# A ninth pair with seven products in the last output projection of a two-layer encoder, its seventh operand block in the distance table's room

## The chip, the cores and the metric

The kernel runs on one core of a Trainium2 chip. The metric is the device time of one execution in microseconds (us). The kernel before ran three times: 2584.67, 2586.02 and 2587.11 us, the median is 2586.02. One further execution was profiled; it took 2583.95 us, of which the profile's span covers 2581.8.

## What is computed

Two layers (DEPTH = 2) work on 256 tokens with 4096 features. A layer normalises x, projects it with w_in (4096 x 11264), runs attention and retention heads on the result and projects their 4096 outputs with w_out (4096 x 4096) onto x:

```python
for l in range(DEPTH):
    h = rmsnorm(x, norm_w[l])
    proj = h @ w_in[l]
    ...
    x = x + jnp.concatenate([a_out, r_out], axis=-1) @ w_out[l]
return rmsnorm(x, final_norm)
```

The four projections are called phases 0 to 3 here. Phase 3, the last w_out, is the one that the change touches. It is followed only by the residual, the final norm and the store.

## The kernel before, in words

**Pairs and products.** The 4096 rows of a weight are 32 tiles of 128, taken as 16 pairs (0 to 15). A pair times a block of 2 x 512 columns is a 2 x 2 product of blocks (two weight tiles, two halves of the tokens, two column blocks of 512). It is done either with eight block products or, by Strassen's scheme in Winograd's form, with seven. Each block product is three matmuls of 128 x 128 by 512 columns, since every operand is split into a high and a low part: high by high, high weight by low operand, low weight by high operand. The banks M1 to M7 in PSUM collect the products over all pairs of a block; at its end a few VectorE additions (`combining`, tiles `ca` and `cb`) turn them into the output. Phase 3 has four blocks of 1024 columns, called blocks 0 to 3 here. `SEVEN_OUT` (L157) lists the pairs that take seven products in w_out: the even ones, eight of 16.

**What a pair needs.** Its weights come from HBM by SyncE as two transfers of 512 KB into `wraw` (6 buffers). A pair with eight products makes two pages, A and B, of 1024 columns each: ScalarE casts the high part (`whi<-wraw`), VectorE subtracts for the low part (`wlo<-wraw,whi`). Page B of most of them is "far": ScalarE makes `fhi` and the negated `flo`, and a GpSimd transfer adds the weight to `flo`, so that VectorE does nothing for it. A pair with seven products makes four pages, A, T, B, U. T and U are sums of weights that VectorE builds first (`wsum`, one instruction of 1024 columns, then two of 512), and VectorE makes the low parts of all four (`wlo` of 1024 columns for A, T, U, and `wlb` of 512 for B). There are 3 buffers for `wlo`, 4 for `whi`, 2 for `wsum`, one for `whb`/`wlb`.

**The order within a block** (`groups_of`, `pages_of`). A group is a pair with seven products and the pairs with eight that follow it; the pages of both alternate. With the even pairs on seven, each group is one seven and one eight.

**Operands.** The activations of a pair are split once per phase (`split_pair`) into tiles `x7h`/`x7l` (7 blocks of 128 columns), `x8h`/`x8l` (6 blocks, 8 buffers, given out in turn) or `xmh`/`xml` for pair 14. In phase 3 the splits of the later pairs run during block 0, together with the rest of the retention work of layer 1.

**The late pairs and the tail.** `LATE` (L195) is the last four pairs below 15 with eight products: 7, 9, 11 and 13. In block 3 their M4 products are put off to the very end (`rest_units`), 24 matmuls, so that the other banks can be combined meanwhile. The half page that is kept for this lies in the `x8` or `x7` buffer of an earlier pair that is through. When pair `LATE_PAIR` = 5 (L61) and all before it are through in block 3, `after` starts the loads that only the tail needs: two rows of `final_norm` into `x8h` and `x8l`, the buffers after the two that pair 7's half pages took (pair 5's own), and then, in `residuals`, two residual blocks of 512 KB into `wsum`. `last_combining` waits for both residuals before it adds anything but M1, M6 and M7.

**Order of the work.** A recording layer runs through the whole program when it is built, with a clock of its own, and writes down each engine's instruction order. On the chip each engine runs its list strictly in that order and waits on semaphores. `dist` (L431) is a table of token distances that the retention weights read (L1404, L1406), for the last time in phase 2.

Of the kernel before, what the change touches and what calls it, by code (L numbers as in the profile page):

```python
# [12 lines left out]
F32R = mybir.dt.float32r  # L13
# [5 lines left out]
P = 128  # L19
D_MODEL = 4096  # L20
SEQ = 256
DEPTH = 2
# [13 lines left out]
ALL = slice(None)  # L36
# [27 lines left out]
PE_PASS = 0.2  # L64
# [91 lines left out]
SEVEN_IN = (0,2,4,6,8,10,12)  # L156
SEVEN_OUT = (0, 2, 4, 6, 8, 10, 12, 14)  # L157
FAR_IN=(1,3,5,7,9,11,13)
FAR_OUT = (1, 3, 5, 7, 9, 11, 13)
SEVENS = (SEVEN_IN, SEVEN_OUT) * DEPTH  # L160
BORDER_FAR = 10


def fars(phase, b):

    few = (FAR_IN, FAR_OUT)[phase % 2]
    if (b == 0 and phase) or (phase % 2 == 0 and b == N_IN - 1):
        eights = [_p for _p in range(NP) if _p not in SEVENS[phase]]
        return few + tuple(_p for _p in eights if _p not in few)[: BORDER_FAR - len(few)]
    return few  # L170


SEVEN_ALWAYS = sum(_p in SEVEN_IN and _p in SEVEN_OUT for _p in range(NP))
EIGHT_ALWAYS = sum(_p not in SEVEN_IN and _p not in SEVEN_OUT for _p in range(NP))
MIXED = tuple(_p for _p in range(NP) if (_p in SEVEN_IN) != (_p in SEVEN_OUT))
# [47 lines left out]
class Now:  # L223

    t = 0.0
# [121 lines left out]
def hybrid_encoder(  # L347
# [17 lines left out]
    ve = Clock(nc.vector, vector_cost, 0.083, now)  # L365
    ac = Clock(nc.scalar, scalar_cost, 0.098, now)
    pe = Clock(None, None, PE_PASS - PASS, now)
# [8 lines left out]
    cp = ctx.enter_context(tc.tile_pool(name="cp", bufs=1))  # L376
# [14 lines left out]
    def t(pool, shape, tag, bufs=None, dt=F32):  # L391
        kw = {} if bufs is None else {"bufs": bufs}
        return pool.tile(shape, dt, tag=tag, name=tag, **kw)

    def f32(v):
        return v.bitcast(F32)
# [9 lines left out]
    def drop(n=1):  # L406

        held[0] -= n
        own(-n)
# [8 lines left out]
    def page(shape, name, dt=F32):  # L418

        held[0] += 1  # L420
        own(1)
        assert held[0] <= PAGES, (name, now.t, [(v.steps.__name__, v.need, v.own, v.begun) for v in tasks], pledged(), wanted, sums_of)
        return sp.tile(shape, dt, tag="pg", name=name, bufs=PAGES)
# [7 lines left out]
    dist = t(cp, [P, 2 * SEQ], "dist", dt=mybir.dt.bfloat16)  # L431
# [334 lines left out]
    weights = Weights()  # L766
# [157 lines left out]
    operand = [None] * NP  # L924
# [5 lines left out]
            need_at.setdefault((g.phase, g.pair), g.at)  # L930
    plain, plain_left = {}, list(DIRECT)
    late, stored, sums_of, split_of = [], {}, [], {}

    def split_pair(p, v, phase, gains):

        def tokens(v):

            return v.rearrange("p k (a t) -> p k a t", t=BLK)

        x0, x1 = v[:, 0], v[:, 1]  # L940
        if gains is not None:
            yield "A"
            for i in range(2):
                u = v[:, :, i].rearrange("p m a t -> p (a m) t" if phase else "p m a t -> p m (a t)")
                ac.activation(u, u, AF.Copy, scale=gains[i])
        seven = p in SEVENS[phase]
        tag, n = ("xm", len(MIXED)) if p in MIXED else ("x7", SEVEN_ALWAYS) if seven else ("x8", EIGHT_ALWAYS)
        blocks = 6 if tag == "x8" else 7
        if seven:
            yield lambda: not sums_of and held[0] + sum(max(0, v.need - v.own) for v in tasks if v.begun) < PAGES  # L950
            sums_of.append(p)
            hi, lo = (t(ap, [P, blocks, P], tag + s, n, F32R) for s in "hl")
            f = page([P, 5, P], "xf")
            yield "A"
            s1, s2, s3, s4, a22n = (tokens(f)[:, i - S4] for i in (S1, S2, S3, S4, A22N))
            ac.activation(a22n, x1[:, 1], AF.Copy, scale=-1.0)
            ac.copy(tokens(hi[:, 0:2, :]), x0)
            yield "V"
            ve.tensor_sub(s1, a22n, x1[:, 0])
            ve.scalar_tensor_tensor(s2, s1, -1.0, x0[:, 0], op0=ALU.mult, op1=ALU.subtract)  # L960
            ve.tensor_sub(s3, x0[:, 0], x1[:, 0])
            ve.tensor_sub(s4, x0[:, 1], s2)
            yield "A"
            ac.copy(hi[:, 2:7, :], f)
            yield "V"
            ve.tensor_sub(tokens(lo[:, 0:2, :]), x0, tokens(f32(hi)[:, 0:2, :]))
            ve.tensor_sub(lo[:, 2:7, :], f, f32(hi)[:, 2:7, :])
            sums_of.pop()
            drop()
        else:  # L970
            hi, lo = (t(ap, [P, blocks, P], tag + s, n, F32R) for s in "hl")
            u = [w[:, :4].rearrange("p (i m) (a t) -> p i m a t", i=2, t=BLK) for w in (hi, lo)]
            g = [tokens(w[:, 4:6]) for w in (hi, lo)]
            yield "A"
            for i in range(2):
                ac.copy(u[0][:, i], v[:, :, i])
            yield "V"
            for i in range(2):
                ve.tensor_sub(u[1][:, i], v[:, :, i], f32(u[0])[:, i])
            ve.tensor_sub(x0, x0, x1)  # L980
            yield "A"
            ac.copy(g[0], x0)
            yield "V"
            ve.tensor_sub(g[1], x0, f32(g[0]))
        split_of[p // 2] -= 1
        if not split_of[p // 2]:
            drop()
        version[p] = phase
        operand[p] = (hi, lo)
        operand_at[p] = max(ve.done, ac.done)  # L990
# [188 lines left out]
    def at(parts, *index):  # L1179
        return [v[index] for v in parts]  # L1180
# [394 lines left out]
    def block(after_pair, phase, first_order=False, order=LAST_ORDER, last=None):  # L1575
# [37 lines left out]
        for n, (p, k, (bank, index, h), part) in enumerate(units):  # L1613
            if n == len(units) - COMBINE_LEAD:
                wanted[0] = 2
            while (p, k) not in pages:
                g = weights.pages[weights.at]
                weights.at += 1
                assert g.phase == phase
                pages[g.pair, g.kind] = g  # L1620
            g = pages[p, k]

            def ready():
                if part == "D":
                    return (
                        weights.has(g, "raw")
                        and p in plain
                        and plain[p][2 if index[1] == 2 else 1] <= now.t
                        and (n != first[bank] or bank_at[bank] is not None and bank_at[bank] <= now.t)
                    )  # L1630
                when = g.high_at if part == "H" else g.low_at
                if when is None or not (when() if callable(when) else when <= now.t) or version[p] != phase or operand_at[p] > now.t:
                    return False
                return n != first[bank] or (bank_at[bank] is not None and bank_at[bank] <= now.t)

            yield ready
            if n == first[bank]:
                acc[bank] = t(pm, [P, NB], bank)
                bank_at[bank] = None
            if part == "D":  # L1640
                a = None
            elif g.seven:
                a = at(operand[p], *index, ALL)
            else:
                a = at(operand[p], ALL, 4 + index[0] if index[1] == 2 else 2 * index[0] + index[1], ALL)
            if part == "D":
                matmul(acc[bank], plain[p][0][index], f32(g.raw[0])[:, h], n == first[bank], n == final[bank], 4)
            elif part == "H":
                b = g.hi if k == PAGE_B and g.seven else g.hi[h] if last and p in LATE else g.hi[:, h]
                matmul(acc[bank], a[0], b, n == first[bank], False)  # L1650
                matmul(acc[bank], a[1], b, False, False)
            else:
                b = g.lo if k == PAGE_B and g.seven else g.lo[h] if last and p in LATE else g.lo[:, h]
                matmul(acc[bank], a[0], b, False, n == final[bank])
            if n == final[bank]:
                fin[bank] = pe.done
            if n < len(units) - len(rest_units):
                uses[p, k] -= 1
                if not uses[p, k]:
                    weights.release(g)  # L1660
            left[p] -= 1
            if not left[p]:
                done.append(p)
                if last and p not in MIXED and p < NP - 1:
                    weights.holds["x7" if g.seven else "x8"].give(pe.until + PE_PASS)
                if part == "D":
                    plain_left.remove(p)
            while done and all(not left[q] for q in range(min(done))):
                q = min(done)
                done.remove(q)  # L1670
                after_pair(q)
# [378 lines left out]
```

## Time and profile before

| | us |
|---|---|
| median of 3 runs | 2586.02 |
| profiled execution | 2583.95 |
| its span | 2581.8 |
| TensorE busy | 2564.9 |
| VectorE busy | 2317.7 |
| ScalarE busy | 1911.4 |
| GpSimd busy | 443.8 |

"Busy" sums the times in which an engine has an instruction in flight; instructions of one engine overlap a little, so a busy share near 100% can also mean that the next one always starts at once. In a timeline a row is start, duration, engine, source line, instruction, and in brackets the idle time before it and what ended it. L1170 is the line of every matmul and L248 that of every recorded VectorE and ScalarE instruction, so the tiles tell them apart.

### The profile page before, as it was taken

To read this page: it belongs to the slowest core of one execution; us is meant where nothing else is said; L and a number is where in the kernel's file an instruction comes from. 1 tells how busy PE (TensorE), PEld (TensorE's weight loads), DVE (VectorE), ACT (ScalarE), POOL (GpSimd) and SP (SyncE) were. 2 spreads that over 40 slices of the span, in tenths; PEclk is the share of its full clock that TensorE was granted. 3 is DMA by queue.
4 is the path that set the end of the run, shared out by engine and by line. 5 is a ranking of instruction groups with operands and counts; after the bars stand their busy time and mean duration, and the time that the engine had idled before them with its cause. 6 is when DMAs were issued, how large, how long until landed. Compare 5 with 4: busy or idle time off the path is not lost.

```text
span 2581.8 us, 34363 instructions
## 1 busy us (share of the span) xinstructions
PE 2564.9 (99%) x11474; PEld 2115.2 (82%) x11474; DVE 2317.7 (90%) x2911; ACT 1911.4 (74%) x2680; POOL 443.8 (17%) x604
## 2 busy tenths in 40 slices
PE   9999999999999999999999999999999999999998
PEld 5888888888888888888888888888888888888886
DVE  7999988999889899888998989989989888998887
ACT  8877776777777688766887776767778777876665
POOL 0022211221222110111112121212212111101111
PEclk9999999999999999999999999999999999999999
DMA  9999989998998898999999998989998998989987
GB/s 322 306 281 300 287 274 284 282 303 261 287 289 267 278 287 246 291 289 288 305 304 284 291 283 272 276 284 291 293 272 283 283 281 258 291 247 289 268 264 231
DMA packets 212739, 727.53 MB, mean 282 GB/s; under 512 B 25536, under 2 KB 32320, under 8 KB 212560
## 3 DMA queue, kind: packets, MB, share of 16 engines
q1 hardware_dynamic: 146464, 519.21, 56.8%
q0 software_dynamic: 66096, 206.11, 34.7%
q8 instruction: 90, 1.47, 0.2%
q14 instruction: 89, 0.73, 0.1%
HBM read 676.99 MB, written 48.23 MB: 281 GB/s over the span
## 4 chain that ended last, share of the span: by engine, by line
PE 95%; issue 1%; DVE 1%; DMA 1%; ACT 1%; POOL 0%; SPq 0%; POOLq 0%; DVEq 0%; ACTq 0%
PE M L1170 92%; PE ps L1170 3%; DMA full<-in_xT 0%; DVE wlo L248 0%; DMA flo<-in_w_in 0%; DVE wsum L248 0%; ACT whi L248 0%; DVE cb L248 0%; PE ps L1009 0%; DMA wraw<-in_w_in 0%; DVE ca L248 0%; POOL out L1862 0%; ACT full L248 0%; ACT fhi L248 0%; SPq L372 0%
## 5 line engine op out<-in xcount | busy, mean ns | idle before, releaser
L248 ACT CAST whi<-wraw 128x1024 fp32r<-128x1024 f32 (+1 forms) x521 | 540.2, 1045 | 200.5 <-PE M L1170 128.6
L248 DVE TENSOR_TENSOR wlo<-wraw,whi 128x1024 fp32r<-128x1024 f32 (+1 forms) x521 | 630.0, 1216 | 47.8 <-PE M L1170 20.8
L248 DVE TENSOR_TENSOR wlo<-wsum,whi 128x1024 fp32r<-128x1024 f32 x432 | 527.2, 1221 | 97.0 <-PE M L1170 93.4
L248 ACT CAST whi<-wsum 128x1024 fp32r<-128x1024 f32 x432 | 453.3, 1049 | 151.9 <-PE M L1170 105.4
L1170 PE MATMUL M<-whi,x7h 128*128 128x512 f32 x1248 | 486.6, 390 | 0.0
L1170 PE MATMUL M<-whi,x7l 128*128 128x512 f32 x1248 | 485.7, 389 | 0.0
L1170 PE MATMUL M<-whi,x8h 128*128 128x512 f32 x1048 | 408.2, 389 | 0.0
L1170 PE MATMUL M<-whi,x8l 128*128 128x512 f32 x1048 | 408.0, 389 | 0.0
L1170 PE MATMUL M<-wlo,x7h 128*128 128x512 f32 x1248 | 386.3, 390 | 1.5 <-DVE wlo L248 1.5
L1170 PE MATMUL M<-fhi,x8h 128*128 128x512 f32 x840 | 327.3, 390 | 0.0
L1170 PE MATMUL M<-fhi,x8l 128*128 128x512 f32 x840 | 327.0, 389 | 0.0
L1170 PE MATMUL M<-wlo,x8h 128*128 128x512 f32 x1048 | 309.1, 390 | 1.2 <-DVE wlo L248 1.2
L372 POOL DMA_DIRECT2D flo<-in_w_in x157 | 139.3, 887 | 993.9 <-ACT flo L248 893.7
L248 ACT CAST fhi<-wraw 128x1024 fp32r<-128x1024 f32 (+1 forms) x215 | 224.2, 1043 | 104.3 <-PE M L1170 64.2
L248 DVE TENSOR_TENSOR wsum<-wraw 128x1024 f32<-128x1024 f32 x216 | 263.5, 1220 | 17.1 <-DMA wraw<-in_w_out 8.3
L1170 PEld LDWEIGHTS M<-wlo,x7h 128*128 128x128 f32 x1248 | 233.3, 188 | 50.6 <-DVE wlo L248 3.0
L1170 PEld LDWEIGHTS M<-whi,x7l 128*128 128x128 f32 x1248 | 234.3, 188 | 49.1 <-issue 0.5
L1170 PEld LDWEIGHTS M<-whi,x7h 128*128 128x128 f32 x1248 | 234.3, 188 | 49.1 <-issue 0.2
L248 ACT ACTIVATE flo<-fhi 128x1024 fp32r<-128x1024 f32 (+1 forms) x215 | 226.5, 1054 | 8.3 <-ACT fhi L248 1.7
L1170 PEld LDWEIGHTS M<-wlo,x8h 128*128 128x128 f32 x1048 | 196.3, 188 | 42.9 <-DVE wlo L248 2.4
L1170 PEld LDWEIGHTS M<-whi,x8l 128*128 128x128 f32 x1048 | 196.8, 188 | 40.6
L1170 PEld LDWEIGHTS M<-whi,x8h 128*128 128x128 f32 x1048 | 196.8, 188 | 40.5 <-ACT whi L248 0.3
(280 smaller groups left out, 3784.9 us busy)
## 6 DMA issues: line engine op xcount, KB each, us to landing
wraw<-in_w_in SPq DMA_DIRECT2D x703, 512.0 KB, 6.0
wraw<-in_w_out SPq DMA_DIRECT2D x256, 512.0 KB, 6.4
flo<-in_w_in POOLq DMA_DIRECT2D x157, 512.0 KB, 8.6
flo<-in_w_out POOLq DMA_DIRECT2D x54, 512.0 KB, 8.7
full<-next_dram POOLq DMA_DIRECT2D x18, 512.0 KB, 10.2
p_dram<-room POOLq DMA_DIRECT2D x64, 128.0 KB, 3.4
pT<-p_dram POOLq DMA_DIRECT2D x16, 512.0 KB, 9.9
next_dram<-room POOLq DMA_DIRECT2D x40, 128.0 KB, 5.9
```

The lines of the kernel that those rows point to most:

```text
L248: return call(out, *args, **kwargs)
L372: getattr(nc, name).dma_start(to, src, **kw)
L1170: nc.tensor.matmul(out, a, b, start=start, stop=stop)
```

## The change

`SEVENS` gives phase 3 alone a ninth pair with seven products, pair 7 (`EXTRA`). Pair 7 keeps its `x8h`/`x8l` buffer, which has six blocks, so the seventh operand block, high and low, goes into a tile `more` that takes the room of `dist`.

```diff
 FAR_OUT = (1, 3, 5, 7, 9, 11, 13)
-SEVENS = (SEVEN_IN, SEVEN_OUT) * DEPTH
+EXTRA = 7
+SEVENS = (SEVEN_IN, SEVEN_OUT) * (DEPTH - 1) + (SEVEN_IN, tuple(sorted(SEVEN_OUT + (EXTRA,))))
...
-    few = (FAR_IN, FAR_OUT)[phase % 2]
+    few = tuple(_p for _p in (FAR_IN, FAR_OUT)[phase % 2] if _p not in SEVENS[phase])
...
-        tag, n = ("xm", len(MIXED)) if p in MIXED else ("x7", SEVEN_ALWAYS) if seven else ("x8", EIGHT_ALWAYS)
+        tag, n = ("xm", len(MIXED)) if p in MIXED else ("x7", SEVEN_ALWAYS) if p in SEVEN_IN else ("x8", EIGHT_ALWAYS)
...
             hi, lo = (t(ap, [P, blocks, P], tag + s, n, F32R) for s in "hl")
+            if p == EXTRA:
+                more = t(cp, [P, 2, P], "dist", dt=F32R)
...
-            ac.copy(hi[:, 2:7, :], f)
+            ac.copy(hi[:, 2:blocks, :], f[:, : blocks - 2])
+            if p == EXTRA:
+                ac.copy(more[:, 0], f[:, 4])
             yield "V"
             ve.tensor_sub(tokens(lo[:, 0:2, :]), x0, tokens(f32(hi)[:, 0:2, :]))
-            ve.tensor_sub(lo[:, 2:7, :], f, f32(hi)[:, 2:7, :])
+            ve.tensor_sub(lo[:, 2:blocks, :], f[:, : blocks - 2], f32(hi)[:, 2:blocks, :])
+            if p == EXTRA:
+                ve.tensor_sub(more[:, 1], f[:, 4], f32(more)[:, 0])
+                seventh.append([more[:, 0], more[:, 1]])
...
-                a = at(operand[p], *index, ALL)
+                a = seventh[0] if p == EXTRA and index[1] == 6 else at(operand[p], *index, ALL)
...
-                    weights.holds["x7" if g.seven else "x8"].give(pe.until + PE_PASS)
+                    weights.holds["x7" if p in SEVEN_IN else "x8"].give(pe.until + PE_PASS)
```

`LATE` is computed from `SEVENS` and is not in the diff: with pair 7 among the sevens it becomes 5, 9, 11 and 13. `LATE_PAIR` stays 5. Pairs 6 and 7 are now groups of one pair each, so their eight pages stand one after another with no page of a pair with eight products between them. The VectorE list grows from 2911 to 2938 instructions, the TensorE list loses 12 matmuls.

Where the change moves instructions, at three places:

VectorE in block 0 of phase 3, around pair 7. Before, from the low part of pair 6's page A on: the two `wsum` rows are pair 6's page U, the `wlo` from `wraw_20849` is all that pair 7 asks for (its page A), the next `wlo` is pair 6's page T, and the last rows are retention work of layer 1.

```order
L248 TENSOR_TENSOR wlo_20948<-wraw_20767,whi_20903 128x1024
L248 TENSOR_TENSOR wsum_20963<-wraw_20767,wsum_20923 128x512
L248 TENSOR_TENSOR wsum_20963<-wsum_20963,wraw_20794 128x512
L248 TENSOR_TENSOR wlo_20973<-wraw_20849,whi_20915 128x1024
L248 TENSOR_TENSOR wlo_20987<-wsum_20923,whi_20945 128x1024
L248 SCALAR_TENSOR_TENSOR cb_20495<-tanh_20959,cb_20495 128x512
L248 TENSOR_TENSOR cb_20495<-cb_20495,o_20346 128x512
```

Now, from pair 7's first sum on (`wraw_20802` and `wraw_20841` are its weights, `wsum_20955` and `whi_20974` are pair 6's page U, `wraw_20880` belongs to pair 8):

```order
L249 TENSOR_TENSOR wsum_20987<-wraw_20802,wraw_20841 128x1024
L249 TENSOR_TENSOR wlo_21000<-wsum_20955,whi_20974 128x1024
L249 TENSOR_TENSOR wlo_21008<-wraw_20802,whi_20992 128x1024
L249 TENSOR_TENSOR wsum_21018<-wraw_20802,wsum_20987 128x512
L249 TENSOR_TENSOR wsum_21018<-wsum_21018,wraw_20841 128x512
L249 TENSOR_TENSOR wlo_21027<-wsum_20987,whi_21004 128x1024
L249 TENSOR_TENSOR wlb_21041<-wraw_20841,whb_21016 128x512
L249 TENSOR_TENSOR wsum_21045<-wraw_20880,wraw_20918 128x1024
L249 TENSOR_TENSOR wlo_21056<-wsum_21018,whi_21031 128x1024
```

Pair 7 has seven instructions where it had one: three of 1024 columns and three of 512 are new.

SyncE at the end of the program. Before, the two `final_norm` rows (`x8h`, `x8l`) stand ahead of the last ten weight loads, and the residuals (`wsum`) behind them:

```order
L372 DMA x8h<-in_final_norm 128x512
L372 DMA x8l<-in_final_norm 128x512
L372 DMA wraw<-in_w_out 128x1024 x2
L372 DMA gain<-in_final_norm 128x512
L372 DMA wraw<-in_w_out 128x1024 x8
L372 DMA wsum<-x_dram 128x1024 x2
L1862 DMA out<-ca 128x512 x8
```

Now (with what each waits for):

```order
L373 DMA wraw<-in_w_out 128x1024 [waits DMAHW6_49,DVE_49,Activation_49]
L373 DMA x8h<-in_final_norm 128x512 [waits PE_49]
L373 DMA x8l<-in_final_norm 128x512 [waits DMAHW7_49]
L373 DMA wsum<-x_dram 128x1024 [waits DMAHW0_49,DVE_49]
L373 DMA wsum<-x_dram 128x1024 [waits DMAHW1_49,DVE_49]
```

The two `final_norm` rows now stand behind the last weight load, the residuals stay behind them, and the first of the four waits for TensorE.

TensorE at the start of the 24 last matmuls (M4 of the late pairs). Before, the first six read pair 7's operand (`x8h_20566`, `x8l_20567`):

```order
L1170 MATMUL M4_22878<-x8h_23080,x8h_20566 128x512
L1170 MATMUL M4_22878<-x8h_23080,x8l_20567 128x512
L1170 MATMUL M4_22878<-x8l_23099,x8h_20566 128x512
L1170 MATMUL M4_22878<-x8h_23022,x8h_20566 128x512
L1170 MATMUL M4_22878<-x8h_23022,x8l_20567 128x512
L1170 MATMUL M4_22878<-x8l_23024,x8h_20566 128x512
L1170 MATMUL M4_22878<-x7h_23177,x8h_20650 128x512
```

Now they read pair 5's (`x8h_20362`, `x8l_20363`):

```order
L1179 MATMUL M4_22911<-x8h_23052,x8h_20362 128x512
L1179 MATMUL M4_22911<-x8h_23052,x8l_20363 128x512
L1179 MATMUL M4_22911<-x8l_23064,x8h_20362 128x512
L1179 MATMUL M4_22911<-x8h_22965,x8h_20362 128x512
L1179 MATMUL M4_22911<-x8h_22965,x8l_20363 128x512
L1179 MATMUL M4_22911<-x8l_22967,x8h_20362 128x512
L1179 MATMUL M4_22911<-x7h_23222,x8h_20639 128x512
```

So pair 5 is not through before the sixth of these 24 matmuls, and its `x8h`/`x8l` buffers are the ones that the `final_norm` rows take.

More of the change, by code (lines that the diff above doesn't have):

```diff
@@ L932, in hybrid_encoder @@
     late, stored, sums_of, split_of = [], {}, [], {}
+    seventh = []
     def split_pair(p, v, phase, gains):
```

## The prediction

> **What bounds the kernel now.** I read the head of the profile's page first, then the chain of waits, then the windows of phase 3 by block, since the change touches only that phase.
>
> ```profile
> span 2581.8 us, 34363 instructions
> PE 2564.9 (99%) x11474; PEld 2115.2 (82%) x11474; DVE 2317.7 (90%) x2911; ACT 1911.4 (74%) x2680; POOL 443.8 (17%) x604
> ...
> 2280.41 255.29 PE M L1170 x1126
> ```
>
> TensorE (PE) is the bound: 99% of the span, and the chain runs through phase 3 as one unbroken piece of 1126 matmuls in 255.29 us, 0.2267 us each. So a matmul less is worth 0.23 us, but only where TensorE does not then wait for something else. The windows below are the four blocks and the tail; the columns are busy time and count of each engine, granted TensorE clock, DMA share and GB/s.
>
> ```profile
> 2241.00:2324.00 83.00, 83.00 (x375) 68.72 (x374) 81.88 (x118) 67.75 (x97) 6.85 (x8) 1.00 0.88 247
> 2324.00:2406.00 82.00, 82.00 (x363) 67.89 (x363) 69.83 (x76) 55.66 (x65) 8.56 (x10) 1.00 0.91 275
> ...
> 2488.00:2560.00 72.00, 72.00 (x319) 59.39 (x318) 63.71 (x71) 48.14 (x70) 9.54 (x11) 1.00 0.88 263
> 2560.00:2582.00 22.00, 9.63 (x43) 7.65 (x41) 12.06 (x26) 6.79 (x14) 5.58 (x10) 0.78 0.52 192
> ```
>
> VectorE (DVE, the third pair of numbers) is at 81.88 of 83 us in block 0, because the splits of the operands and the retention work run beside the weights there. In the next blocks it has 12 us free in 82. In the last 22 us TensorE works only 9.63: there something else sets the end.
>
> **The sevens for eights.** Each of the four blocks has one product less of three matmuls: 12 matmuls, 12 x 0.2267 = **-2.72 us** (-0.68 a block). This is the whole gain. GpSimd loses four accumulating transfers (three far half pages fewer in blocks 0 to 2, one in block 3); it is busy 6.85 to 9.54 us in these windows, so that is worth nothing. The `dist` room costs nothing either: its last reader is in phase 2. ScalarE (fourth pair) has 14 to 26 us free per block, which covers its new casts.
>
> **VectorE in block 0.** Pair 7 as an eight asks VectorE for one low part of 1024 columns. As a seven it adds one `wsum` of 1024, two of 512, two more `wlo` of 1024 and a `wlb` of 512. What such instructions cost in block 0, and what one pair's split costs:
>
> ```profile
> L248 DVE TENSOR_TENSOR wlo<-wsum,whi 128x1024 fp32r<-128x1024 f32 x16 | 19.5, 1221 | 0.3 <-PE M L1170 0.2
> L248 DVE TENSOR_TENSOR wsum<-wraw 128x1024 f32<-128x1024 f32 x8 | 9.8, 1220 | 0.0
> L248 DVE TENSOR_TENSOR wsum<-wsum,wraw 128x512 f32<-128x512 f32 x8 | 5.5, 692 | 0.3
> L248 DVE TENSOR_TENSOR wlb<-wraw,whb 128x512 fp32r<-128x512 f32 x7 | 4.8, 684 | 0.0
> L248 DVE TENSOR_TENSOR x8l<-full,x8h 128x256 fp32r<-128x256 f32 x7 | 2.8, 420 | 0.0
> L248 DVE TENSOR_TENSOR xf<-xf,full x25: 283/286/289, 12.2 to 2260.5; 128x128 f32<-128x128 f32 x25
> ...
> 2268.05 1.22 DVE L248 TENSOR_TENSOR wlo<-wsum,whi 128x1024 fp32r<-128x1024 f32 x1
> 2269.19 1.22 DVE L248 TENSOR_TENSOR wlo<-wraw,whi 128x1024 fp32r<-128x1024 f32 x1
> 2270.33 0.69 DVE L248 TENSOR_TENSOR wsum<-wraw,wsum 128x512 f32<-128x512 f32 x1
> 2271.05 0.69 DVE L248 TENSOR_TENSOR wsum<-wsum,wraw 128x512 f32<-128x512 f32 x1
> 2271.65 1.22 DVE L248 TENSOR_TENSOR wlo<-wraw,whi 128x1024 fp32r<-128x1024 f32 x1
> ```
>
> The idle column (0.0 to 0.3 us over the block) says that VectorE waits for nobody, so every new instruction pushes all behind it. In the timeline the starts of such a queue follow 1.14 us apart (1024 columns) and 0.72 or 0.60 (512), less than the rows' 1.22 and 0.69. I take those: 3 x 1.14 + 0.72 + 2 x 0.60 = 5.34 us. The split of pair 7 as an eight is four instructions of 256 (4 x 0.42 = 1.7); as a seven it is four of 128 (4 x 0.29), one of 256, one of 512 (0.69, the nearest row) and one of 128: 1.14 + 0.42 + 0.69 + 0.29 = 2.5. That is +0.8, together +6.1. In the order of the changed kernel two `ca` additions of 512 columns, which stood behind block 1's first low part (pair 0's page A), now stand ahead of it: 2 x 0.65 = +1.3. So that low part comes **7.4 us** later on VectorE.
>
> The Trainium skill, "VectorE: DVE Perf Modes", section "The DRAIN you can't avoid", says that an instruction does not start before the pipe of the one ahead is empty. By that rule each new instruction would cost its full row, 0.4 us more over the six; the starts above, 1.14 us apart on rows of 1.22, do not bear it out as a full price here.
>
> How much of this TensorE feels depends on how early the low parts are:
>
> ```profile
> 2317.52 1.22 DVE L248 TENSOR_TENSOR wlo<-wraw,whi 128x1024 fp32r<-128x1024 f32 x1
> 2323.29 1.22 DVE L248 TENSOR_TENSOR wlo<-wraw,whi 128x1024 fp32r<-128x1024 f32 x1
> ...
> 2319.51 0.39 PE L1170 MATMUL M<-wlo,x8h 128*128 128x512 f32 x1
> 2325.41 0.62 PE L1170 MATMUL M<-wlo,x7h 128*128 128x512 f32 x2
> ```
>
> Pair 15's low part, the last of block 0, ends at 2318.74 and is used at 2319.51, 0.77 us later. The next, block 1's first, ends at 2324.51 and is used at 2325.41, 0.90 us later. That is all the slack that block 0 has at its end. TensorE starts block 1's low products 7.4 - 0.9 = **+6.5 us** later, and block 0's own -0.68 is lost in that, since VectorE sets the time. The bounds: +3 if VectorE drops or reorders about half of it into its gaps (it had 83.00 - 81.88 = 1.1 us of them in the window) and the leads further forward, +8 if the rows count in full.
>
> **Blocks 1 to 3.** VectorE has 12 us to spare, of which the six new instructions take the same 5.34. But pairs 6 and 7 are now two sevens with nothing between them. A seven takes VectorE 4 x 1.14 + 0.72 + 2 x 0.60 = 6.5 us and TensorE 21 x 0.2267 = 4.8, so the two leave VectorE 3.4 us behind. Against that stands the lead with which it arrives at pair 6:
>
> ```profile
> 2340.10 1.23 DVE L248 TENSOR_TENSOR wsum<-wraw 128x1024 f32<-128x1024 f32 x1 [2.17 <-DMA wraw<-in_w_out]
> 2352.97 1.22 DVE L248 TENSOR_TENSOR wlo<-wraw,whi 128x1024 fp32r<-128x1024 f32 x1
> 2432.39 1.22 DVE L248 TENSOR_TENSOR wlo<-wraw,whi 128x1024 fp32r<-128x1024 f32 x1
> ...
> 2356.01 0.61 PE L1170 MATMUL M<-wlo,x7h 128*128 128x512 f32 x2
> 2437.61 0.61 PE L1170 MATMUL M<-wlo,x7h 128*128 128x512 f32 x2
> ```
>
> In block 1 the low part of pair 6's page A is ready 2356.01 - 2354.19 = 1.8 us early (VectorE had lost 2.17 us to a weight load at 2340.10), in block 2 it is 2437.61 - 2433.61 = 4.0 us early. So block 1 should stall by 3.4 - 1.8 = 1.6 us and blocks 2 and 3 hardly; I take **+2.0** for the three, with 0 and +5 as ends (nothing if the weights are there earlier, once block 0's delay has let the loads run ahead; 5 if each of the three stalls by half of its deficit), beside **-2.04** for their matmuls.
>
> **The tail.** The four loads that only the end needs now hang on pair 5, whose last products are among the final 24 matmuls:
>
> ```profile
> 2519.26 0.42 SPq L372 DMA_DIRECT2D x8h<-in_final_norm  x1
> 2519.73 0.44 SPq L372 DMA_DIRECT2D x8l<-in_final_norm  x1
> ...
> 2554.87 2.06 SPq L372 DMA_DIRECT2D wsum<-x_dram  x2
> ...
> wsum<-x_dram SPq DMA_DIRECT2D x2, 512.0 KB, 3.4
> x8h<-in_final_norm SPq DMA_DIRECT2D x1, 256.0 KB, 8.7
> ...
> 2565.39 0.39 PE L1170 MATMUL M<-x7h,x8h 128*128 128x512 f32 x1
> ...
> 2560.09 0.69 DVE L248 TENSOR_TENSOR ca<-ca,wsum 128x512 f32<-128x512 f32 x1
> 2562.87 0.69 DVE L248 TENSOR_TENSOR cb<-cb,M 128x512 f32<-128x512 f32 x1 [0.31 <-PE M L1170]
> ```
>
> Before, the two `final_norm` loads were issued at 2519 and the residuals at 2554.87; these landed about 3.4 us after their issue, and VectorE's first residual addition started at 2560.09. Now the first of the four waits until TensorE is through with the first six of the 24. In the clock of before the seventh starts at 2565.39. SyncE then issues the two `final_norm` rows (0.42 + 0.44) and the residuals behind them: 2566.3 at the earliest, landed 3.4 us later, 2569.7. Ahead of them are the 512 KB of the two rows, at 263 GB/s (the window's rate) 2.0 us if nothing overlaps; I take 0.7 of it, so the first addition starts at 2570.4 in place of 2560.09, **+10.3**. VectorE's list behind it keeps its order; the 0.31 us that it waited for TensorE at 2562.87 falls away, since TensorE will be ahead, so **+10.0**. The ends: +8 if the residuals, which no longer share the queues with the last weights, land 1.3 us sooner and do not wait for the two rows, +14.5 if `final_norm` takes the 8.7 us that it took beside the weight stream. TensorE is done before VectorE in either, so the tail's time is added to the end in full.
>
> **The sum**, against the profiled execution: +6.5 (block 0, its own gain inside) - 2.04 + 2.0 + 10.0 = **+16.5 us**; span 2581.8 to 2598.3. The profiled execution took 2583.95, 2.07 below the median of the runs, so the difference is laid on the median: 2586.02 + 16.5 = **2602.5 us**.
>
> **The rivals.** *Only TensorE counts:* VectorE's new work fits into its leads, and the loads are off the path as they were. Then the time is 2586.02 - 2.72 = 2583.3, not slower. Against it: 0.0 to 0.3 us of idle time in block 0 with under 1 us of lead, and 2560.09 against a load that cannot leave before 2565. Chance 3%. *Block 0 stalls, the tail does not:* the loads come to lie behind something that ended later anyway. Then +6.5 - 2.04 + 2.0 = 2592.5. Against it: the window of the tail has VectorE idle for 10 of 22 us, mostly after its chain, and none of it ahead of the residuals. 10%. *The tail stalls, block 0 does not:* the leads in mid-block are longer than at its end, and VectorE might run further ahead with new buffers free. Then -2.72 + 2.0 + 10.0 = 2595.3. 12%. *More stalls than I count:* VectorE is late at each pair of sevens by its whole deficit of 3.4 us (10.2 in place of 2.0), with the same block 0 and tail: +24.7, 2610.7. For it: at 2340.10 VectorE waited 2.17 us for a weight load, so the loads are near the edge, and a late VectorE gives their buffers back late. Against it: 12 us of free time a block. 15%.
>
> To this last one belongs the clock, 1.00 in all windows of the blocks and 0.78 in the tail, where TensorE works 9.63 of 22 us. The Trainium skill, "TensorE: Matmul & The Clock Gate", section "HAM oscillation — how this bites in real kernels", warns that gaps of a few microseconds in TensorE's work can bring the clock down to half. Were one stall long enough, the work after it would run slower for a while; the row of the tail agrees that gaps and a lower clock go together, and whether a single gap of 2 to 6 us suffices no run here shows yet.
>
> **How the numbers follow.** The forecast has 60% (its own range, 2597 to 2608, from the ends of its terms), the rivals 3, 10, 12 and 15. The range of 8 in 10 runs from 2593 to 2609: it leaves out the first rival, part of the second, and about half of the last. A run's measurement tells about 0.2% (5.2 us) from no change. The one rival that gains has 2.7 us, so most of it lies within: 0.04 with a sliver of the second rival's low end, and faster by over that 0.02, if VectorE's new order should bring something that I don't see. Slower: 0.94.
>
> **What would show it.** In the changed kernel's profile: twelve matmuls less; the VectorE window of block 0 about 6 us longer with no idle time; TensorE idle before `wlo` products at the end of block 0 and the start of block 1, 6 to 7 us in sum, ended by VectorE; a small idle time, up to 2 us, at pairs 6 and 7 of block 1; `x8h`, `x8l` and `wsum` issued only behind the sixth of the last 24 matmuls; and VectorE idle for about 10 us ahead of `ca<-ca,wsum`, ended by a DMA. I am wrong if block 0's last low part is used as early as before, if the residual additions still start within 3 us of TensorE's last phase, or if TensorE's clock falls in the blocks.

## The result, and the profile after

The changed kernel takes 2592.65 us (median of 10 runs, 2590.19 to 2594.20) against 2585.68 us for the kernel before (10 runs on the same chip): ratio 1.0025, 95% interval 1.0017 to 1.0033. That is 7.0 us slower, where 16.5 were forecast. It lies just under the forecast range's low end of 2593.0.

The head of the page of the changed kernel:

```profile
span 2590.9 us, 34376 instructions
PE 2566.3 (99%) x11462; PEld 2113.0 (82%) x11462; DVE 2340.0 (90%) x2938; ACT 1915.5 (74%) x2685; POOL 441.4 (17%) x600
```

The twelve matmuls are gone (11474 to 11462), yet the span is 9.1 us longer. The windows of phase 3, cut at the same times as before (columns: busy time and count of PE, PEld, DVE, ACT, POOL, then clock, DMA share, GB/s):

```profile
2241.00:2324.00 83.00, 79.34 (x350) 63.58 (x349) 81.60 (x120) 67.39 (x97) 6.01 (x7) 1.00 0.81 226
2324.00:2406.00 82.00, 80.41 (x355) 66.17 (x354) 75.43 (x82) 53.98 (x64) 6.89 (x8) 1.00 0.86 263
2406.00:2488.00 82.00, 81.47 (x359) 66.95 (x358) 74.84 (x81) 56.12 (x66) 6.89 (x8) 1.00 0.88 261
2488.00:2560.00 72.00, 72.00 (x318) 59.08 (x317) 67.85 (x78) 49.81 (x72) 9.53 (x11) 1.00 0.91 270
2560.00:2582.00 22.00, 17.10 (x76) 13.83 (x74) 19.69 (x34) 10.23 (x19) 3.82 (x7) 0.98 0.39 135
```

TensorE, which was busy for the whole of the first three windows before, now lacks 3.66, 1.59 and 0.53 us in them. VectorE stands at 81.60 of 83 us in block 0, as before: it was full, and the new work could only make it later. In the blocks behind it went from 70 to 75 us, which still leaves room. The list of waits of phase 3 names who is late (waiter, its releaser: us in total, times, longest), and TensorE's timeline says where (in brackets the idle time and its releaser):

```profile
PEld M L1179 <- DVE wlo L249: 8.0, 8, 2.1
PE M L1179 <- DVE wlo L249: 5.0, 5, 1.7
...
2237.67 0.50 PE L1179 MATMUL M<-flo,x8h 128*128 128x512 f32 x1 [0.22 <-DMA flo<-in_w_in]
...
2295.87 0.74 PE L1179 MATMUL M<-wlo,x7h 128*128 128x512 f32 x2 [0.41 <-DVE wlo L249]
...
2307.76 0.73 PE L1179 MATMUL M<-wlo,x7h 128*128 128x512 f32 x2 [0.84 <-DVE wlo L249]
...
2319.25 0.39 PE L1179 MATMUL M<-whi,xml 128*128 128x512 f32 x1
2321.30 0.73 PE L1179 MATMUL M<-wlo,xmh 128*128 128x512 f32 x2 [1.66 <-DVE wlo L249]
...
2333.41 0.74 PE L1179 MATMUL M<-wlo,x7h 128*128 128x512 f32 x2 [1.59 <-DVE wlo L249]
...
2454.18 0.73 PE L1179 MATMUL M<-wlo,x8h 128*128 128x512 f32 x2 [0.53 <-DVE wlo L249]
...
2572.86 0.39 PE L1179 MATMUL M<-x7h,x8h 128*128 128x512 f32 x1
```

All of TensorE's waits for `wlo` but one lie between 2295 and 2334. (PEld is TensorE's weight load, which overlaps the matmuls.) A wait costs more than its idle column: the matmul at 2321.30 starts 2.05 us after the one at 2319.25, where 0.23 is usual, and its idle time reads 1.66, since the row ahead lasts 0.39 us. The kernel before has the first and the last of these instructions at

```profile
2236.51 0.50 PE L1170 MATMUL M<-flo,x8h 128*128 128x512 f32 x1
```

and 2565.39, and block 1's first low product at 2325.41. So the 9.1 us of the span fall apart as follows:

| stretch | at its end, against before | its share | forecast |
|---|---|---|---|
| up to the start of phase 3 (no change there) | +1.2 (2236.51 to 2237.67) | +1.2 | 0 |
| block 0, to block 1's first low product | +8.0 (2325.41 to 2333.41) | **+6.8** | +6.5 |
| blocks 1 to 3, to the seventh of the last 24 matmuls | +7.5 (2565.39 to 2572.86) | **-0.5** | 0 |
| tail, to the end of the span | +9.1 (2581.8 to 2590.9) | **+1.6** | +10.0 |

The first line is a difference between two executions (TensorE's list is the same up to there), so the profile gives 7.9 us to the change and the medians 7.0. In the profiles of the other kernels below phase 3 starts between 2236.4 and 2241.9, so that line is noise of single executions, and a span alone can't be compared.

At the border of blocks 0 and 1 VectorE's list reads as the order had it: pair 15's low part, then the sums and the bank additions, the two `ca` additions last, and only then the low part that TensorE waits for at 2333.41:

```profile
2324.04 1.22 DVE L249 TENSOR_TENSOR wlo<-wraw,whi 128x1024 fp32r<-128x1024 f32 x1
...
2330.94 1.28 DVE L249 TENSOR_TENSOR ca<-ca,M 128x512 f32<-128x512 f32 x2
2332.13 2.35 DVE L249 TENSOR_TENSOR wlo<-wraw,whi 128x1024 fp32r<-128x1024 f32 x2
```

Before, the two `ca` additions stood behind that low part, which started at 2323.29:

```profile
2324.43 1.28 DVE L248 TENSOR_TENSOR ca<-ca,M 128x512 f32<-128x512 f32 x2
```

The tail, from the timelines of SyncE, TensorE and VectorE:

```profile
2547.72 4.37 SPq L373 DMA_DIRECT2D wraw<-in_w_out  x2
2552.14 0.59 SPq L373 DMA_DIRECT2D x8h<-in_final_norm  x1
2552.78 0.56 SPq L373 DMA_DIRECT2D x8l<-in_final_norm  x1
2562.35 2.06 SPq L373 DMA_DIRECT2D wsum<-x_dram  x2
...
2571.50 0.39 PE L1179 MATMUL M<-x8h 128*128 128x512 f32 x1
...
2563.98 2.35 DVE L249 TENSOR_TENSOR wlo<-wraw,whi 128x1024 fp32r<-128x1024 f32 x2
2566.25 1.22 DVE L249 TENSOR_TENSOR cb<-cb,gain 128x1024 f32<-128x1024 f32 x1
2567.60 0.69 DVE L249 TENSOR_TENSOR cb<-ca,M 128x512 f32<-128x512 f32 x1
2568.93 0.68 DVE L249 TENSOR_TENSOR ca<-ca,wsum 128x512 f32<-128x512 f32 x1
```

The two `final_norm` rows leave at 2552.14, 0.05 us after the last weight load (2547.72 + 4.37), and 19 us before the first of the 24 last matmuls at 2571.50. They do not wait for pair 5. The residuals leave at 2562.35, and the first addition of one (2568.93) follows the instruction ahead of it without idle time. What is new in the tail is one product by `gain` (1.22 us) between the last low part and the first bank addition. Before, it had its place well ahead of them:

```profile
2535.50 1.22 DVE L248 TENSOR_TENSOR cb<-cb,gain 128x1024 f32<-128x1024 f32 x1
```

### The profile page after: what moved, and what is told of

The parts are those of the page before. It is cut to its first block, busy times and chain, and to the rows that moved or that the text cites. A ratio compares the mean times of both kernels' runs of the same rounds, so it can differ in the third digit from the quotient of the medians.

```text
span 2590.9 us, 34376 instructions
## 1 busy us (share of the span) xinstructions
PE 2566.3 (99%) x11462; PEld 2113.0 (82%) x11462; DVE 2340.0 (90%) x2938; ACT 1915.5 (74%) x2685; POOL 441.4 (17%) x600
## 4 chain that ended last, share of the span: by engine, by line
PE 92%; DVE 3%; DMA 2%; ACT 1%; issue 1%; POOL 0%; SPq 0%; POOLq 0%; DVEq 0%; ACTq 0%
PE M L1179 89%; PE ps L1179 3%; DVE wlo L249 2%; DMA wraw<-in_w_out 1%; DVE wsum L249 1%; DVE cb L249 1%; DMA flo<-in_w_in 1%; ACT whi L249 0%; DMA wraw<-in_w_in 0%; DMA full<-in_xT 0%; DVE ca L249 0%; ACT full L249 0%; ACT fhi L249 0%; PE ps L1018 0%; DVE x7l L249 0%
## 5 line engine op out<-in xcount | busy, mean ns | idle before, releaser
L249 DVE TENSOR_TENSOR wlo<-wsum,whi 128x1024 fp32r<-128x1024 f32 x440 | 536.5, 1220 | 90.2 <-PE M L1179 85.5
L249 ACT CAST whi<-wsum 128x1024 fp32r<-128x1024 f32 x440 | 461.9, 1050 | 160.8 <-PE M L1179 103.8
L1179 PE MATMUL M<-fhi,x8h 128*128 128x512 f32 x824 | 320.9, 389 | 0.0
L1179 PE MATMUL M<-fhi,x8l 128*128 128x512 f32 x824 | 320.8, 389 | 0.0
```

Of the source, the lines that this page charges most:

```text
L249: return call(out, *args, **kwargs)
L1179: nc.tensor.matmul(out, a, b, start=start, stop=stop)
```

## The experiments

Each kernel was timed in five rounds beside the kernel before on the same chip (5 to 11 executions of each, 11 to 27 of the kernel before). The theory that the profile suggests: the loss is VectorE's work in block 0, and nothing else. The rivals: the tail (what the prediction gave 10 us to), the two sevens in a row, and an order at the end that costs by itself.

**The tail alone.** The kernel before, with the late pairs of the changed kernel:

```diff
-LATE = tuple(_p for _p in range(NP - 1) if _p not in SEVENS[2 * DEPTH - 1])[-LATE_PAIRS:]
+LATE = (5, 9, 11, 13)
```

> The kernel before with the late pairs 5, 9, 11, 13 in place of 7, 9, 11, 13, nothing else. The tail's loads then stand behind the last weight load, as in the changed kernel. If the rows of final_norm take the buffer of pair 7, which is through early (what the changed kernel's trace suggests), the time stays: 0, within 1 us. If they wait for pair 5's last products, as the prediction had it: +10 us, about 2596.

2585.97 against 2586.16 us, ratio 0.9999 (0.9990 to 1.0008). The `final_norm` rows now stand behind the last weight load here too, and leave at once (SyncE's timeline):

```profile
2535.38 9.39 SPq L372 DMA_DIRECT2D wraw<-in_w_out  x5
2544.82 0.45 SPq L372 DMA_DIRECT2D x8h<-in_final_norm  x1
```

The new place of the loads costs nothing: the 10 us of the prediction have no cause.

**VectorE's work alone.** The kernel before, with five low parts made twice (the second writes the same values), in block 0 and in another kernel in block 2:

```diff
...
                 ve.tensor_sub(lo, v, f32(hi))
+                if g.phase == 2 * DEPTH - 1 and g.block == 0 and g.kind == PAGE_T and g.pair in (4, 6, 8, 10, 12):
+                    ve.tensor_sub(lo, v, f32(hi))
```

> The kernel before with five low parts of 1024 columns (page T of pairs 4, 6, 8, 10, 12) made twice in block 0 of phase 3: about 5.7 us more for VectorE, no matmul less, same output. By the VectorE theory (block 0 has no slack beyond 0.9 us) the time rises by 5 to 6 us, TensorE waiting late in block 0. If it is the pair of sevens or the tail that costs, 0.

> The same five instructions doubled in block 2, where VectorE has 12 us free. By the VectorE theory 0, within 1 us; if any further instruction on VectorE costs its time (or makes the chip slower as a whole), about +5.7 us as in block 0.

In block 0: 2594.53 against 2586.16 us, ratio 1.0034 (1.0021 to 1.0046), 8.4 us. In block 2: 2585.56 us, ratio 1.0000 (0.9991 to 1.0009). The first window is block 0 with its doubled instructions, the second block 2 with its own:

```profile
2241.00:2324.00 83.00, 80.24 (x357) 64.87 (x355) 81.64 (x121) 65.47 (x96) 7.73 (x9) 1.00 0.85 243
...
2406.00:2488.00 82.00, 82.00 (x363) 67.83 (x363) 75.72 (x80) 55.75 (x64) 7.89 (x10) 1.00 0.92 270
```

The same 5.7 us of work cost TensorE its time where VectorE is full (81.64 of 83) and nothing where it ends at 75.72 of 82. This alone, with no seven, no new order of the tail and no matmul less, is as slow as the change. Cut at the same three matmuls as in the table above, its profile has the loss in block 0 alone (the table below): +6.2 us there, where 5.7 of new work and 1.3 of the two `ca` additions, which stand ahead of block 1's first low part here too, less 0.9 of lead make 6.1.

**Taking work away.** The eight instructions of the retention gate that VectorE makes in block 0, left out of the kernel before and of the changed kernel:

```diff
         for m in range(MT):
             yield "V"
+            if L.index == DEPTH - 1:
+                continue
             ve.scalar_tensor_tensor(acc[:, m, :], e[:, m, :], 1.0, acc[:, m, :], op0=ALU.add, op1=ALU.mult)
             ve.tensor_mul(acc[:, m, :], acc[:, m, :], o[:, m, :])
```

> The kernel before without the eight retention gate instructions of VectorE in the last layer (the gate's tanh and product are left out), which stand in block 0: 5 to 6 us less for VectorE. TensorE has no wait there before the change, so 0, within 1 us. A control for the same cut in the changed kernel.

> The changed kernel without the same eight retention gate instructions (the gate is left out): VectorE has 5.3 us less in block 0 up to block 1's first low part. By the VectorE theory TensorE's waits in block 0 shrink from about 7 to 2 us and the time is 5 us below the changed kernel's, about 2587 to 2588 against 2586 of before. If block 0's VectorE is not the cause, it stays at 2592 to 2593.

Before: 2585.74 against 2586.16 us, ratio 0.9996 (0.9987 to 1.0005), so nothing. Changed: 2587.14 against 2586.10 us, ratio 1.0004 (0.9996 to 1.0013), 5.5 us under the changed kernel's 2592.65. What is left of TensorE's waits on VectorE from 2241 to 2345 is the one at block 1's first low part:

```profile
PE M L1179 <- DVE wlo L249: 1.6, 1, 1.6
```

A third kernel also leaves out four additions at the end of block 0 (`light` is true there), and with them that wait:

```diff
...
+            if light and b != "M5":
+                pass
-            if b == "M5":
+            elif b == "M5":
```

> The changed kernel without the eight retention gate instructions and without four of the additions that empty the banks of block 0 (the gate, and M3, M2 and M4 of block 0, are left out): VectorE's list up to block 1's first low part is 91.7 us, 7.2 us shorter than the changed kernel's and level with the kernel before. By the VectorE theory the last stall (1.7 us at block 1's first low part) goes too, and what is left of the change is its 2.7 us of products less what the tail costs (up to 1.6): 2584 to 2586. If it stays at 2587 or over, something else in the change costs time.

2585.20 against 2586.06 us, ratio 0.9997 (0.9988 to 1.0006). With VectorE's list for block 0 as long as before, the change costs nothing. The gain that is left by the medians, 0.9 us, is too small to be shown by them, but its profile (the table below) has it in place: -0.3 us in block 0, -1.5 in blocks 1 to 3, +1.0 in the tail. The twelve products bring 1.8 us here and not 2.7.

**Another pair.** Pair 3 in place of pair 7. The late pairs are then the old ones:

```diff
-EXTRA = 7
+EXTRA = 3
```

> The changed kernel with pair 3 in place of pair 7 as the ninth seven. The late pairs and the loads of the tail are then as before. By the VectorE theory about the same stall, since the same instructions are new in block 0: +6 to +9 us over before. If the changed late pairs (pair 5 for 7) cost the time, 0 to -2.

2595.86 against 2586.10 us, ratio 1.0038 (1.0026 to 1.0050), 9.8 us, with the tail as before. The waits from 2241 to 2370:

```profile
PE M L1179 <- DVE wlo L249: 8.1, 7, 1.7
...
PE M L1179 <- ACT whb L249: 1.5, 1, 1.5
```

So the loss goes with the ninth seven and not with the late pairs. It is larger than pair 7's by the medians, though the two intervals overlap; in its profile block 0 loses 8.9 us and blocks 1 to 3 lose 3.0, the wait on ScalarE (at 2348.02) among them.

**Mending it.** Four kernels try to keep the change and lose the stall. The product by `gain` ahead of the last low parts:

```diff
+ ... due=0.0 if last_layer and n == N_OUT2 - 2 else ...
```

> The changed kernel with the last product by gain taken ahead of the weights' low parts, so that it does not stand in the tail between the last low part and the last additions. If it costs there what its row shows, -1.1 to -1.3 us against the changed kernel (about 2591.4); 0 if the tail waits for TensorE or the residuals anyway.

2593.09 against 2586.10 us, ratio 1.0026 (1.0016 to 1.0035): no gain. VectorE is then late in block 3 instead, as the waits from 2488 to the end say; in the changed kernel TensorE had not waited there:

```profile
PE M L1179 <- DVE wlo L249: 1.9, 2, 1.3
```

So the product is what the tail had lost by: the tail falls from +1.6 to -0.2 us against before, and blocks 1 to 3 rise from -0.5 to +0.9.

Low parts of the next block ahead of the bank additions:

```diff
+        w = weights.best(e)
+        if e == "V" and phase_now[0] == 2 * DEPTH - 1 and w and w.key < weights.place() + 3.0:
+            weights.make(w)
+            clear()
+            return True
         if step_lane(e, urgent):
```

> The changed kernel with the low parts of the next block ahead of the additions that empty the banks, at the borders of the blocks of phase 3. Block 1's first low part then stands 4.5 us earlier in VectorE's list. By the VectorE theory the stall at that border (1.9 us) goes and some of the stall ahead of it; -2 to -4 us against the changed kernel. If TensorE then waits for the banks instead: 0 or slower.

2594.92 against 2586.10 us, ratio 1.0032 (1.0020 to 1.0044). The stall did not go, it moved: the rule also puts low parts ahead of the splits of the later pairs, and TensorE waits for their operands (it has no wait at block 1's first low part any more, and that part is used no earlier). TensorE's timeline, and a window behind it:

```profile
2296.71 0.50 PE L1184 MATMUL M<-whi,x7l 128*128 128x512 f32 x1 [1.50 <-DVE x7l L249]
...
2299.01 0.62 PE L1184 MATMUL M<-whi,x8h 128*128 128x512 f32 x1 [0.60 <-ACT x8h L249]
2299.84 0.79 PE L1184 MATMUL M<-whi,x8l 128*128 128x512 f32 x1 [0.22 <-DVE x8l L249]
...
2299.00:2303.00 4.00, 3.77 (x9) 2.72 (x10) 3.93 (x11) 1.94 (x3) 0.00 (x0) 0.57 1.04 261
```

The gate's four products on GpSimd, in the last layer alone (GpSimd is busy 6 us of 83 there):

```diff
-            ve.tensor_mul(acc[:, m, :], acc[:, m, :], o[:, m, :])
+            if L.index == DEPTH - 1:
+                nc.gpsimd.tensor_tensor(acc[:, m, :], acc[:, m, :], o[:, m, :], op=ALU.mult)
...
```

> The changed kernel with the four gate products (ca and cb times the retention output, 128 x 512 each) made by GpSimd in place of VectorE in the last layer; same output. VectorE's list up to block 1's first low part is 2.6 us shorter. By the VectorE theory -2 to -3 us against the changed kernel, about 2590, if GpSimd's products come in time for the splits behind them and do not slow VectorE. If GpSimd takes several us for each and the splits wait, or the two engines hinder each other, 0 or slower.

2594.25 against 2586.03 us, ratio 1.0033 (1.0022 to 1.0044): no gain. The timelines of GpSimd and of VectorE say why:

```profile
2267.83 3.89 POOL L1516 TENSOR_TENSOR ca<-ca,o 128x512 f32<-128x512 f32 x2 [11.32 <-DVE ca L249]
...
2268.26 2.32 DVE L249 TENSOR_TENSOR wsum<-wraw 128x1024 f32<-128x1024 f32 x1
2270.50 2.30 DVE L249 TENSOR_TENSOR wlo<-wsum,whi 128x1024 fp32r<-128x1024 f32 x1
```

While GpSimd makes its two products (3.89 us), the two VectorE instructions beside them take 2.32 and 2.30 us in place of 1.22: 2.2 us more, for two products of 0.69 saved. Beside the other two products a 0.68 us row becomes 1.78 and a 1.22 us row 2.32.

Low parts of page A by an accumulating transfer, as those of page B are, for three pairs and for five:

```diff
+ ... or (phase == 2 * DEPTH - 1 and b == 0 and k == PAGE_A and p in (9, 11, 13))
...
-            for _, lo, v in self.each(g, g.src[1]):
+            for _, lo, v in self.each(g, g.src[int(g.kind == PAGE_B)]):
```

> The changed kernel with the low parts of page A of pairs 9, 11 and 13 in block 0 of phase 3 made by ScalarE and an accumulating transfer, as page B's are, in place of VectorE; same output. VectorE's list up to block 1's first low part is 6.0 us shorter (92.9 against 98.9; 91.5 in the kernel before). By the VectorE theory the stall in block 0 nearly goes: about 5 us under the changed kernel, 2587 to 2588. If three more transfers in the two buffers come too late for TensorE, or ScalarE (some 3 us more) becomes late, 2590 or more.

> The same for pairs 3, 5, 9, 11 and 13: VectorE's list up to block 1's first low part is 8.3 us shorter than the changed kernel's (90.6) and 0.9 us shorter than that of the kernel before. By the VectorE theory no stall on VectorE is left and the products saved show: 2584 to 2586, level with the kernel before or just under it. If the transfers come late, TensorE waits for flo and the time is at or over the changed kernel's.

2593.60 (ratio 1.0030, 1.0019 to 1.0042) and 2592.46 us (1.0026, 1.0016 to 1.0035) against 2586.18. VectorE no longer holds TensorE up at the end of block 0; the transfer does. TensorE in block 0 with three such pairs:

```profile
2307.67 1.20 PE L1179 MATMUL M<-flo,x8h 128*128 128x512 f32 x4 [1.88 <-DMA flo<-in_w_out]
2314.48 1.20 PE L1179 MATMUL M<-flo,x8h 128*128 128x512 f32 x4 [0.40 <-DMA flo<-in_w_out]
2319.85 1.20 PE L1179 MATMUL M<-flo,x8h 128*128 128x512 f32 x4 [0.98 <-DMA flo<-in_w_out]
```

The pair of sevens shows too, in block 1 at pair 7. With five pairs (with three the two waits are 0.34 and 0.52 us), VectorE's wait for a weight load ahead of them first:

```profile
2352.99 1.23 DVE L249 TENSOR_TENSOR wsum<-wraw 128x1024 f32<-128x1024 f32 x1 [2.16 <-DMA wraw<-in_w_out]
...
2367.68 0.50 PE L1179 MATMUL M<-wlo,x8h 128*128 128x512 f32 x1 [0.53 <-DVE wlo L249]
...
2370.55 0.73 PE L1179 MATMUL M<-wlo,x8h 128*128 128x512 f32 x2 [0.52 <-DVE wlo L249]
```

No version with the full computation and the ninth seven was faster than the kernel before.

**The same cut for the kernels that bear on the cause.** The first four columns are the starts of the three matmuls and the span, the last three what each stretch has more than in the kernel before. Each is one execution: the product by `gain` moves nothing in block 0, and its kernel differs there by 0.8 us from the changed one.

| kernel | phase 3 | block 1's first low product | seventh of the last 24 | span | block 0 | blocks 1 to 3 | tail |
|---|---|---|---|---|---|---|---|
| before | 2236.51 | 2325.41 | 2565.39 | 2581.8 | | | |
| changed | 2237.67 | 2333.41 | 2572.86 | 2590.9 | +6.8 | -0.5 | +1.6 |
| before, low parts doubled in block 0 | 2241.89 | 2337.01 | 2577.13 | 2593.6 | +6.2 | +0.1 | +0.1 |
| changed, no gate | 2238.70 | 2329.03 | 2567.70 | 2585.1 | +1.4 | -1.3 | +1.0 |
| changed, no gate, four additions less | 2241.67 | 2330.30 | 2568.74 | 2586.1 | -0.3 | -1.5 | +1.0 |
| changed, pair 3 for pair 7 | 2236.38 | 2334.18 | 2577.16 | 2593.8 | +8.9 | +3.0 | +0.2 |
| changed, product by `gain` earlier | 2238.01 | 2332.88 | 2573.74 | 2589.9 | +6.0 | +0.9 | -0.2 |

## Why the prediction was right in part and wrong in sum

- **The products, -2.72.** The twelve matmuls are gone, as forecast. The kernel without a stall in block 0 stands at 0.9997 (0.9988 to 1.0006); its profile has 0.3 us less in block 0 and 1.5 less in blocks 1 to 3, where 0.68 and 2.04 were forecast. So they are worth about two thirds of the term, by one execution.
- **Block 0, +6.5.** Right: +6.8. The place (the end of block 0 and block 1's first low part), the releaser and the sum (6.1 us of new work, 1.3 from the two `ca` additions, less 0.9 of slack) came out. The doubled low parts show the mechanism without the change, and leaving work out shows it in the change. The four waits at the chosen rows are 0.41 to 1.66 us; the first fall as early as 2295, so the lead is used up there already, well before the end of the block. The statement on VectorE's start-to-start prices held, too: 1.14 us per instruction of 1024 columns made the right sum.
- **Blocks 1 to 3, 0.** Measured -0.5, and the nearness to 0 is in part luck, since both terms were too large: the products bring 1.3 to 1.5 us in the two kernels that leave work out (forecast 2.04), and of the 2.0 us of stalls expected at pairs 6 and 7 one wait came, 0.53 us of idle time, in block 2 and not in block 1. The forecast took VectorE's lead in block 1 from a profile in which it lost 2.17 us to a weight load there. In the changed kernel, and in the two that leave work out, VectorE waits for no weight load at that place, and TensorE doesn't stall; this is the lower end of the prediction's own range (the weights are there earlier), but it does not need block 0's delay, as the kernel without one shows. With the transfers VectorE loses 2.6 and 3.2 us to weight loads there, and the stalls come. That this is the cause is not shown: with the gate's products on GpSimd VectorE loses 2.3 us there too, and TensorE doesn't stall.
- **The tail, +10.0: this step failed.** The prediction, and the section on the change, took it that the two `final_norm` rows go into pair 5's buffers, because the eight `x8` buffers were thought to be given out in a fixed turn. They go to a buffer that is free by then. Before, that was pair 5's; now pair 5 is late and pair 7 is not, and in the built program the rows have the addresses of pair 7's operands, which TensorE reads for the last time at 2534.22, 18 us before the loads leave. The wait for TensorE in SyncE's list is real, but on a matmul long past. The listing showed that a wait was there, not on which instruction; reading its count in the built program would have told. The kernel with the tail alone shows 0 (0.9999).
- **What the tail does cost** is 1.6 us in the profiled execution, and the prediction had nothing of it: one product by `gain` now stands behind the last low part. From its start to that of the next row are 1.35 us (2566.25 to 2567.60); the 0.31 us for which VectorE waited for TensorE fall away, as forecast, and the rest, some 0.5 us, comes behind VectorE's last rows, with the stores. Putting the product ahead takes the tail's cost away (-0.2) but did not lower the time, since VectorE has no room in block 3's last pairs either.
- **The sum.** With the tail at nothing the prediction's own terms give 6.5 - 2.04 + 2.0 = 6.5 us, 2592.5, which is what its second rival said (with a chance of 10%); 2592.65 was measured. That these agree to 0.2 us is luck: the stretches are off by +0.3, -0.5 and +1.6 us, and the profile's own sum is 7.9. The rival "more stalls" did not come, and the clock stayed at 1.00 in all blocks of the changed kernel.

## What to carry to other kernels

An instruction on an engine that is full in one stage costs its whole start-to-start price there, less the lead that its consumer still has, and nothing in a stage where the engine has gaps: 5.7 us of VectorE work cost 8.4 us by the medians (6.2 by the profile's block 0) in block 0 and 0 in block 2. So a saving that holds in every block is to be weighed against the one block in which its side work has no room, before its products are counted. And a wait that a listing shows says that there is one, not that it comes late: find the instruction that it counts to before it is given a price.

## What the runs showed of the hardware that was not expected

- VectorE is slower while GpSimd makes products of tiles in SBUF: 1.22 us became 2.32 and 2.30 beside two GpSimd products of 128 x 512 that took 3.89 us together. The four products took 1.40 to 1.97 us each; whether VectorE slows them no run shows. The Trainium skill, "SBUF — State Buffer", section "Who interferes with whom", says that a VectorE instruction with two SBUF inputs contends with a GpSimd instruction that reads SBUF, and names an exclusive lock; the traces agree on the contention. With GpSimd's engine nearly idle, moving work to it gained nothing.
- TensorE's granted clock fell to 0.57 from 2299 to 2303 in the kernel with the low parts ahead, after waits of 1.50, 0.60 and 0.22 us within some 5 us. In the changed kernel single waits of 1.59 and 1.66 us left it at 1.00. So the longest single gap does not tell the two apart; that several close together lowered the clock is a guess. The Trainium skill, "TensorE: Matmul & The Clock Gate", section "HAM oscillation — how this bites in real kernels", speaks of gaps over 3.4 us, and none here was that long.
- The doubled low parts cost 8.4 us by the medians for 5.7 us of new work. The same two `ca` additions, which the order moves there too, are 1.3 us of the difference; the profile has +6.2 us in block 0, and the rest is within the interval of the medians (5.4 to 11.9 us).
